# Sums of the down projection's left operand moved into the MLP's units and stored, its right operand's sums moved to VectorE, embedding stage begun ahead of the last product

## Chip, core and metric

The kernel runs on one core of a Trainium2 chip. The metric is the device time in microseconds (us): the median of three runs of the kernel before is 1584.94 us (1584.51 to 1587.78).

## What is computed

One layer of a bidirectional encoder, 1024 tokens by 1024 channels, everything in float32. What bears on the change is the second half of the layer, the gated MLP and the stage after it that adds the per-layer embedding:

```python
x = x + conv_glu(rmsnorm(x, norm_ffn_g[i]), w_ffn_gate[i], w_ffn_up[i], ffn_conv_w[i], ffn_conv_b[i], w_ffn_down[i])
gate = jax.nn.sigmoid(rmsnorm(x, norm_ple_g[i]) @ w_ple_gate[i])
x = x + (p[i] @ w_ple[i]) * gate
return rmsnorm(x, final_norm_g)

def conv_glu(h, w_gate, w_up, conv_w, conv_b, w_down):
    a, u = h @ w_gate, h @ w_up
    ap = jnp.pad(a, ((0, 0), (1, 1), (0, 0)))
    c = conv_b
    for j in range(3):
        c = c + ap[:, j:j + S] * conv_w[j]
    return (jax.nn.gelu(c, approximate=False) * u) @ w_down
```

The hidden width is 2816, that is 22 tiles of 128.

## The kernel before

**Products.** Every float32 product is made of three matmuls on a high and a low part of each operand (`mm3`). The parts are made by `split_into`: ScalarE copies the high part, then VectorE or GpSimd subtracts it from the source to get the low part (line 149 in every profile row). The MLP's products are cut into two by two blocks and made with seven block products instead of eight: from the left operand's blocks a11, a12, a21, a22 come four sums s1 to s4, from the right operand's blocks b11 to b22 four sums t1 to t4, and the products are a11·b11, a12·b21, s2·t2, s1·t1, s3·t3, s4·b22 and a22·t4. Their results are added up in the end.

**The MLP's units** (`up`, lines 1056 to 1081; `unit`, 967 to 1012). There are 11 pairs of units, each pair making two hidden tiles for all 1024 tokens: a gate unit, whose products go to PSUM banks D, D, S, S, and an up unit, on four banks E. Each unit is seven products of 12 matmuls. In a unit the banks with c22 and c12 are read by VectorE (lines 997 and 1000) before TensorE may add the last two products into the same banks. When an up unit is done, `up_done` (1038 to 1054) multiplies its two tiles by the gates (VectorE for the first half tile, GpSimd for the rest) and stores both to DRAM (`md`).

**The down projection** (`down`, 1225 to 1238; `down_chunk`, 1167 to 1223). Hidden tiles 0 and 1 (the "rest") are multiplied plainly, as four extra parts; the other 20 tiles form five blocks of four tiles. Three chunks are worked off one after the other: the first has the rest and one block (264 matmuls), the second and third have two blocks each (336 matmuls, 48 for each of the seven products). For each block `down_blocks` (1100 to 1135) loads the four a blocks from `md` (two transfers each) and the four b blocks from the weights, and forms the sums when they are asked for (line 1204): s1 to s4 on VectorE, t1 to t4 on GpSimd, all in line 1125. Then each product's two operands are split (`op_of`), the low parts on VectorE, but of the first block's b blocks and of the rest's on GpSimd. Finished banks are added by VectorE into `acc` or into the residual tiles `x` (line 1173), and in the last chunk GpSimd adds `acc` into `x` (1216 to 1220).

**The embedding stage** (`ple`, 1257 to 1353) starts when the down projection is done: for each of eight token tiles a norm, eight transposes, 48 matmuls with the gate weights, 12 with the embedding weights, and the final norm.

**What sets the order.** Each engine works its own queue in order, DMA issues on SyncE's queue (SP) too. The program's text is reordered within limits by a scheduler, and buffers of a pool are handed on when their last reader is done: pool `c` has 15 buffers of 128x1024 (a blocks, the tiles `x`, the units' outputs), pool `d` has 9 (the split operands of the down projection), `raw` has 3, `w` and `w2` hold 6 and 4 (b blocks and t sums). A load waits in SP's queue for its buffer, and all later issues stand behind it.

```python
sums = dict(s3=("a11", "a21", ALU.subtract, "a11"), s1=("a21", "a22", ALU.add, "a21"),
            s2=("a22", "s3", ALU.subtract, None), s4=("a12", "s2", ALU.subtract, "a12"),
            t1=("b12", "b11", ALU.subtract, "b11"), t3=("b22", "b12", ALU.subtract, "b12"),
            t2=("b22", "t1", ALU.subtract, None), t4=("b21", "t2", ALU.subtract, "b21"))
(v if nm[0] == "s" else p).tensor_tensor(out=t, in0=x, in1=y, op=op)
```

## Time and profile before

| | us |
|---|---|
| median of three runs | 1584.94 (1584.51 to 1587.78) |
| the profiled execution | 1580.84 |
| its span, first to last instruction | 1579.1 |
| TensorE busy in the span | 1504.4 (95%) |
| VectorE, ScalarE, GpSimd busy | 1064.5, 644.7, 611.5 |

In the span the MLP's units run from about 780 to 1205 us, the down projection from 1199 to 1446 us, and the embedding stage from there to the end. The matmul rows carry durations with their pipelining, so the time that TensorE needs for a number of matmuls is read from a stretch in which they run without a gap. "Granted clock" (PEclk) is the share of TensorE's full speed that was granted in a stretch. A time in brackets at the end of a timeline row is how long the engine had been idle, and what released it.

### The profile page before, as it was taken

The page shows a single profiled execution, that of the slowest core. Times are in us where ns is not written, and L with a number is a line of the kernel's source. Part 1 is how long each engine was busy: PE and PEld are TensorE (multiplying, and loading weights), DVE is VectorE, ACT ScalarE, POOL GpSimd, SP SyncE. Part 2 cuts the span into 40 slices and gives each one's busy share as a digit, 9 for nine tenths or more (in the row PEclk, how much of TensorE's full clock was granted, in tenths as well). Part 3 has the DMA queues.
Part 4 walks back from the last instruction along what each step waited for, and adds up shares of the span by engine and source line. Part 5 has one row for each costly group of instructions (what it writes and reads, how often), then busy time and mean ns, then how long its engine had stood idle before and what let it go on. Part 6 is the DMA issues. An engine that isn't in the chain of part 4 may idle for free.

```text
span 1579.1 us, 21704 instructions
## 1 busy us (share of the span) xinstructions
PE 1504.4 (95%) x8550; PEld 1294.9 (82%) x8550; DVE 1064.5 (67%) x1567; ACT 644.7 (41%) x1068; POOL 611.5 (39%) x406
## 2 busy tenths in 40 slices
PE   8999999999999996999999999999998989799997
PEld 7979998999799875888778888888886868687886
DVE  7355566564656666857877666666558997976665
ACT  5345535542455255514643333333333323333322
POOL 3120541243105410620577666656657250635000
PEclk9999999999999999999999999999999999899999
DMA  8100011001100110314412232222227515030011
GB/s 247 41 14 14 28 54 41 28 28 41 41 15 28 54 68 27 121 41 146 148 41 94 80 97 87 88 77 80 94 85 282 180 43 184 10 114 20 34 51 41
DMA packets 92488, 118.58 MB, mean 75 GB/s; under 512 B 5232, under 2 KB 65890, under 8 KB 92386
## 3 DMA queue, kind: packets, MB, share of 16 engines
q1 hardware_dynamic: 91954, 116.34, 22.5%
q8 instruction: 67, 1.10, 0.3%
q10 hardware_dynamic: 432, 0.86, 0.2%
q14 instruction: 35, 0.29, 0.1%
HBM read 92.01 MB, written 23.07 MB: 73 GB/s over the span
## 4 chain that ended last, share of the span: by engine, by line
PE 78%; DVE 11%; issue 4%; ACT 4%; POOL 2%; DMA 1%; DVEq 0%; ACTq 0%; POOLq 0%
PE D L156 33%; PE E L156 18%; PE S L156 9%; PE B L156 5%; PE B L495 3%; PE S L687 3%; PE B L657 3%; DVE op L149 2%; ACT e L665 2%; DVE atm L663 1%; PE S L683 1%; DVE mb L1125 1%; PE B L528 1%; DVE x L1173 1%; DVE raw L1125 1%
## 5 line engine op out<-in xcount | busy, mean ns | idle before, releaser
L156 PE MATMUL D<-w,hT 128*128 128x256 f32 x1920 | 254.8, 287 | 0.1
L156 PEld LDWEIGHTS D<-w,hT 128*128 128x128 f32 x1920 | 237.2, 192 | 2.5 <-issue 1.4
L156 PE MATMUL E<-T,S 128*128 128x512 f32 x924 | 217.2, 394 | 2.8 <-DVE S L149 1.4
L156 PEld LDWEIGHTS E<-T,S 128*128 128x128 f32 x924 | 175.1, 190 | 41.3 <-DVE S L149 1.9
L149 POOL TENSOR_TENSOR S<-w,S 128x512 fp32r<-128x512 f32 x119 | 171.6, 1456 | 92.2 <-ACT S L146 71.9
L149 POOL TENSOR_TENSOR w<-raw,w 128x1024 fp32r<-128x1024 f32 x37 | 92.1, 2493 | 275.2 <-ACT w L146 225.3
L156 PE MATMUL E<-op,op 128*128 128x512 f32 x528 | 128.6, 402 | 10.2 <-DVE x L1173 5.6
L156 PE MATMUL D<-hT,w 128*128 128x512 f32 x576 | 137.4, 394 | 0.0
L156 PEld LDWEIGHTS E<-op,op 128*128 128x128 f32 x528 | 102.9, 196 | 34.1 <-DVE x L1173 6.1
L156 PEld LDWEIGHTS D<-hT,w 128*128 128x128 f32 x576 | 106.3, 188 | 24.1 <-issue 2.9
L156 PE MATMUL S<-T,S 128*128 128x512 f32 x528 | 124.2, 389 | 1.0 <-DVE T L149 1.0
L146 ACT ACTIVATE S<-w 128x512 fp32r<-128x512 f32 x121 | 73.2, 624 | 119.2 <-PE S L156 49.5
L156 PEld LDWEIGHTS S<-T,S 128*128 128x128 f32 x528 | 99.1, 188 | 22.0 <-DVE T L149 1.4
L663 DVE TENSOR_REDUCE atm<-B 128x1 f32<-128x1024 f32 x64 | 75.3, 1218 | 42.5 <-PE B L657 42.5
L156 PE MATMUL D<-T,S 128*128 128x512 f32 x396 | 95.1, 391 | 4.1 <-ACT S L146 2.5
L156 PE MATMUL D<-w,osp 128*128 128x512 f32 x384 | 90.8, 393 | 0.0
L156 PEld LDWEIGHTS D<-T,S 128*128 128x128 f32 x396 | 74.0, 188 | 20.1 <-ACT S L146 2.7
L149 POOL TENSOR_TENSOR S<-raw,S 128x512 fp32r<-128x512 f32 x30 | 47.4, 1579 | 99.0 <-ACT S L146 99.0
L665 ACT ACTIVATE e<-B,atm 128x1024 f32<-128x1024 f32 x64 | 70.7, 1111 | 36.1 <-DVE atm L663 36.1
L156 PEld LDWEIGHTS D<-w,osp 128*128 128x128 f32 x384 | 71.1, 188 | 14.6 <-ACT osp L146 0.3
L156 PE MATMUL B<-wg,h 128*128 128x512 f32 x336 | 79.8, 394 | 0.0
L156 PEld LDWEIGHTS B<-wg,h 128*128 128x128 f32 x336 | 62.9, 189 | 13.2 <-ACT h L146 0.2
(290 smaller groups left out, 2768.7 us busy)
## 6 DMA issues: line engine op xcount, KB each, us to landing
md<-ag SPq DMA_DIRECT2D x22, 512.0 KB, 2.7
mb<-md SPq DMA_DIRECT2D x44, 256.0 KB, 3.7
raw<-in_w_in SPq DMA_DIRECT2D x40, 256.0 KB, 3.2
raw<-in_w_ffn_gate SPq DMA_DIRECT2D x20, 512.0 KB, 4.0
w<-in_w_ffn_up SPq DMA_DIRECT2D x20, 512.0 KB, 3.8
x<-in_x SPq DMA_DIRECT2D x16, 512.0 KB, 6.5
raw<-in_w_in SPq DMA_DIRECT2D x12, 512.0 KB, 3.9
w<-in_w_ffn_down SPq DMA_DIRECT2D x10, 512.0 KB, 6.3
```

What stands on the lines that cost most here:

```text
L146: nc.scalar.activation(hi, src, AF.Copy)
L149: (lo_eng or nc.vector).tensor_tensor(out=lo, in0=src, in1=f32(hi), op=ALU.subtract)
L156: m = self.nc.tensor.matmul(out, a, b, start=new and i == 0 and j == 0, stop=i == n - 1 and j == 2, skip_group_check=not new)
L495: nc.tensor.matmul(ps[:, c * 128:(c + 1) * 128], X[:, c * 128:(c + 1) * 128], vw(Y, [[2 * hh, 64 // hh], [1024 + hh, 2], [1, hh]], c * 128 ...
L528: nc.tensor.matmul(kvs[z][:, c * 128:(c + 1) * 128], KT[:, c, :], v[:, c, :], start=True, stop=True)
L657: mm = nc.tensor.matmul(scs[m][:, kk], qs[a][pr, qq], ks[b][pr, kk], start=j == 0, stop=j == 2).ins
L663: nc.vector.tensor_reduce(nm[:, m:m + 1], sc, AX.X, ALU.max, negate=True)
L665: self.last_exp = nc.scalar.activation(em, sc, AF.Exp, bias=nm[:, m:m + 1], accum_out=(s0 if m == 0 else s1)).ins
L683: nc.tensor.transpose(ps[:, i * 128:(i + 1) * 128], e[:, k * 128:(k + 1) * 128], self.ident)
L687: nc.tensor.matmul(po[:, 0:128], wT[:, k, :], v[:, k, :], start=(k == 0), stop=(k == 7))
L1125: (v if nm[0] == "s" else p).tensor_tensor(out=t, in0=x, in1=y, op=op)
L1173: v.tensor_tensor(out=to, in0=bank, in1=to, op=ALU.add)
```

## The change

The hidden tiles are paired otherwise: the two halves of the inner dimension of a block are now the first and second tile of each unit, so that a11 and a21 (first tile, token halves one and two) and a12 and a22 (second tile) all come out of one up unit.

- In `up_done` the units 1 to 10 form s1 to s4 from their own tiles in place, four VectorE subtractions or additions of 128x512 each, and store them beside a11, a12 and a22 in `md`, which has eight blocks of 128x512 for a unit: two stores of 512 KB more, and a11 is stored by itself (256 KB) instead of with a21. In place means that a sum waits for the store of the block it overwrites.
- `down_blocks` loads the seven a and s blocks instead of four, and forms only t1 to t4, on VectorE. All splits of the down projection's operands are on VectorE now.
- The first block's loads are asked for in another order, the rest's a1 and b1 with them; the tiles `x` are loaded behind them.
- In the last chunk GpSimd adds `acc` to `x` right after the product s2·t2, in another order.
- `ple` is a generator: its first part (embedding weights, the first tile's norm and transposes, the second tile's norm, the gate weights) is put into the program ahead of the last product a22·t4; half of the gate weights go into buffers of `w` and `w2` instead of `d`. The first transposes use banks E.

```diff
@@ up_done
-            self.store(out=self.md[2 * j + k], in_=out[k])
+            a11, a21 = out[0][:, 0:512], out[0][:, 512:1024]
+            md = lambda nm, n=1: self.md[j][:, BLOCKS.index(nm):BLOCKS.index(nm) + n, :]
+            if not k:
+                self.store(out=md("a11"), in_=a11)
+                if j == 0:
+                    self.store(out=md("a21"), in_=a21)
+                return
+            a12, a22 = out[1][:, 0:512], out[1][:, 512:1024]
+            self.store(out=md("a12", 2), in_=out[1].rearrange("p (b s) -> p b s", b=2))
+            if j:
+
+                v.tensor_tensor(out=a11, in0=a11, in1=a21, op=ALU.subtract)
+                v.tensor_tensor(out=a21, in0=a21, in1=a22, op=ALU.add)
+                self.store(out=md("s3", 2), in_=out[0].rearrange("p (b s) -> p b s", b=2))
+                v.tensor_tensor(out=a22, in0=a22, in1=a11, op=ALU.subtract)
+                v.tensor_tensor(out=a12, in0=a12, in1=a22, op=ALU.subtract)
+                self.store(out=md("s4", 2), in_=out[1].rearrange("p (b s) -> p b s", b=2))
@@ down_blocks
-        sums = dict(s3=("a11", "a21", ALU.subtract, "a11"), s1=("a21", "a22", ALU.add, "a21"),
-                    s2=("a22", "s3", ALU.subtract, None), s4=("a12", "s2", ALU.subtract, "a12"),
-                    t1=("b12", "b11", ALU.subtract, "b11"), t3=("b22", "b12", ALU.subtract, "b12"),
-                    t2=("b22", "t1", ALU.subtract, None), t4=("b21", "t2", ALU.subtract, "b21"))
+        sums = dict(t1=("b12", "b11", "b11"), t3=("b22", "b12", "b12"), t2=("b22", "t1", None), t4=("b21", "t2", "b21"))
...
-                    (v if nm[0] == "s" else p).tensor_tensor(out=t, in0=x, in1=y, op=op)
+                    v.tensor_tensor(out=t, in0=x, in1=y, op=ALU.subtract)
...
-            return self.op_of(get(nm), p if first and nm[0] == "b" else v)
+            return self.op_of(get(nm), v)
@@ down_chunk
-        ask("s3", "t1", "s1", "t3", "s2", "t2")
+        ask("t1", "t3", "t2", "t4")
         for i in mult(by, "s2", "t2", True):
             add(acc(i), by[i])
-        ask("s4", "t4")
+        if last:
+            for i in (4, 5, 6, 7, 0, 1, 2, 3):
...
+        prod = mult(by, "a22", "t4", False, ("a2", "b1"))
         if last:
...
-        for i in mult(by, "a22", "t4", False, ("a2", "b1")):
+
+            next(last)
+        for i in prod:
             add(xq(i, 1, 0), by[i])
@@ ple
+        nxt = norm(0)
+        hl = []
+        turner(nxt[1], hl)()
+        prev = (0, hl, nxt[0])
+        nxt = norm(1)
+        self.ple_w()
+        gbf = self.gb_load("final_norm_g", self.wf([1024]))
+        early[0] = False
+        yield
```

**Order on VectorE where a gate unit begins**, just after an up unit has ended (`ag` are a unit's outputs, `mu` its running sum, `w` and `raw` the weights of coming units). Before:

```order
L1006 TENSOR_TENSOR ag_9841<-mu_9820,E_9823 128x512
L1010 TENSOR_TENSOR ag_9842<-mu_9820,E_9824 128x512
L958 TENSOR_TENSOR w_10116<-w_10088 128x512
L959 TENSOR_TENSOR w_10116<-w_10089,w_10115 128x512
L994 TENSOR_TENSOR mu_9953<-mu_9953,D_9955 128x512
L997 TENSOR_TENSOR ag_9975<-mu_9953,S_9957 128x512
L953 TENSOR_TENSOR w_10248<-raw_10221,raw_10222 128x512
L954 TENSOR_TENSOR w_10248<-w_10248,raw_10221 128x512
L1000 TENSOR_TENSOR ag_9975<-ag_9975,S_9956 128x512
```

Of the change, at the same place of the same pair:

```order
L1008 TENSOR_TENSOR ag_9873<-mu_9852,E_9855 128x512
L1012 TENSOR_TENSOR ag_9874<-mu_9852,E_9856 128x512
L1066 TENSOR_TENSOR ag_9873<-ag_9873 128x512
L960 TENSOR_TENSOR w_10154<-w_10126 128x512
L961 TENSOR_TENSOR w_10154<-w_10127,w_10153 128x512
L996 TENSOR_TENSOR mu_9991<-mu_9991,D_9993 128x512
L1067 TENSOR_TENSOR ag_9873<-ag_9873,ag_9874 128x512
L999 TENSOR_TENSOR ag_10013<-mu_9991,S_9995 128x512
L1069 TENSOR_TENSOR ag_9874<-ag_9874,ag_9873 128x512
L1070 TENSOR_TENSOR ag_9874<-ag_9874 128x512
L1002 TENSOR_TENSOR ag_10013<-ag_10013,S_9994 128x512
```

The four sums (lines 1066 to 1070) stand between the gate unit's own reads of its banks (lines 996, 999 and 1002 now).

**Order on VectorE where the second chunk begins** (`op` are split operands, `mb` a blocks, `wf` and `w` b blocks and t sums). Before:

```order
L1125 TENSOR_TENSOR mb_11081<-mb_11081,mb_11095 128x1024
L1125 TENSOR_TENSOR raw_11107<-mb_11095,mb_10936 128x1024
L1125 TENSOR_TENSOR mb_11003<-mb_11003,raw_11105 128x1024
L149 TENSOR_TENSOR op_11011<-wf_11009,op_11011 128x1024
L1173 TENSOR_TENSOR x_10528<-D_10767,x_10528 128x512
L149 TENSOR_TENSOR op_11017<-mb_11014,op_11017 128x1024
L1173 TENSOR_TENSOR x_10530<-D_10768,x_10530 128x512
```

Of the change:

```order
L1144 TENSOR_TENSOR w_10996<-wf_11134,w_10996 128x1024
L151 TENSOR_TENSOR op_11065<-wf_11063,op_11065 128x1024
L1197 TENSOR_TENSOR x_10569<-D_10812,x_10569 128x512
L151 TENSOR_TENSOR op_11071<-mb_11068,op_11071 128x1024
L1144 TENSOR_TENSOR wf_11134<-w_11140,wf_11134 128x1024
L1144 TENSOR_TENSOR wf_11145<-w_11140,w_10996 128x1024
L1197 TENSOR_TENSOR x_10571<-D_10813,x_10571 128x512
L1144 TENSOR_TENSOR wf_11063<-wf_11063,wf_11143 128x1024
```

The s sums are gone from here and the t sums (line 1144) stand in their place, between the splits and the reads of banks D.

**Order on SP where the first chunk runs** (`raw_10561` and `raw_10622` are the rest's b1 block; `md_113` is the last unit's store). Before, the last unit's two stores and then the next chunk's blocks:

```order
L167 DMA raw_10622<-in_w_ffn_down 128x2x512
L1232 DMA x_10532<-xd_93 128x1024
L1232 DMA x_10534<-xd_94 128x1024
L1097 DMA mb_10616<-md_103 128x512
L1097 DMA mb_10616<-md_104 128x512
L161 DMA md_123<-ag_10400 128x1024
L161 DMA md_124<-ag_10401 128x1024
L1097 DMA mb_10925<-md_109 128x512
```

Of the change:

```order
L1260 DMA x_10583<-xd_90 128x1024
L169 DMA raw_10561<-in_w_ffn_down 128x2x512
L163 DMA md_113<-ag_10444 128x512
L163 DMA md_113<-ag_10445 128x1024
L163 DMA md_113<-ag_10444 128x1024
L163 DMA md_113<-ag_10445 128x1024
L1118 DMA mb_10734<-md_104 128x512
L1118 DMA mb_10734<-md_105 128x512
L1118 DMA mb_10775<-md_104 128x512
```

The first block's s2 (`mb_10734`) is issued behind the last unit's four stores, the last of which holds its s4 and s2.

## Rows read from the trace of the kernel before

**Rows 1.** Busy time by stretch in the down projection; columns in the first line.

```profile
core 0: us, PE busy (x) PEld busy (x) DVE busy (x) ACT busy (x) POOL busy (x), PEclk, DMA share, GB/s
1198.59:1445.74 247.15, 227.31 (x963) 184.56 (x961) 212.19 (x184) 79.84 (x80) 108.67 (x42) 0.95 0.35 119
...
1272.26:1294.85 22.59, 15.97 (x58) 12.31 (x57) 22.59 (x15) 6.02 (x6) 12.53 (x5) 0.85 0.01 2
...
1358.10:1381.76 23.66, 15.08 (x59) 11.49 (x57) 23.66 (x17) 6.03 (x6) 12.57 (x5) 0.81 0.05 17
```

**Rows 2.** The chain in order of time, down projection and embedding stage: start, us, work.

```profile
1295.02 10.88 PE E L156 x48
...
1465.44 0.87 PE S L1343 x8
1466.32 1.38 PE D L156 x6
```

**Rows 3.** Timeline where the second and third chunks begin: start, us, engine, instruction, [idle].

```profile
1272.70 3.27 POOL L1125 TENSOR_TENSOR wf<-w,wf 128x1024 f32<-128x1024 f32 x1
...
1273.63 3.42 DVE L1125 TENSOR_TENSOR raw<-mb,mb 128x1024 f32<-128x1024 f32 x1
...
1282.13 9.57 PE L156 MATMUL E<-op,op 128*128 128x512 f32 x30 [5.63 <-DVE x L1173]
...
1379.46 2.50 PE L156 MATMUL D<-op,op 128*128 128x512 f32 x5 [5.89 <-DVE op L149]
```

**Rows 4.** Line 1125, all its instructions: count, ns shortest/median/longest, first and last start.

```profile
L1125 DVE TENSOR_TENSOR mb<-mb,mb x10: 1224/2225/3416, 1203.4 to 1356.2; 128x1024 f32<-128x1024 f32 x10
L1125 DVE TENSOR_TENSOR raw<-mb,mb x5: 1216/3383/3424, 1223.3 to 1359.5; 128x1024 f32<-128x1024 f32 x5
L1125 DVE TENSOR_TENSOR mb<-mb,raw x5: 1205/3317/3427, 1226.8 to 1373.8; 128x1024 f32<-128x1024 f32 x5
...
L1125 POOL TENSOR_TENSOR wf<-w,w x4: 3319/3382/3396, 1264.8 to 1361.8; 128x1024 f32<-128x1024 f32 x4
```

**Rows 5.** Timeline from the last up unit to the rest's product a1·b1.

```profile
1200.18 5.78 PE L156 MATMUL E<-T,S 128*128 128x512 f32 x24
...
1217.79 1.06 ACT L146 ACTIVATE op<-mb 128x1024 fp32r<-128x1024 f32 x1 [18.56 <-DMA mb<-md]
...
1219.84 2.07 PE L156 MATMUL E<-op,op 128*128 128x512 f32 x4 [3.69 <-ACT op L146]
...
1222.39 11.95 PE L156 MATMUL E<-op,op 128*128 128x512 f32 x44 [0.47 <-POOL op L149]
```

**Rows 6.** Timeline from the last product to the first gate matmuls.

```profile
1451.63 1.97 PE L1343 MATMUL S<-cst,c 128*128 128x128 f32 x8 [2.48 <-DVE c L200]
...
1453.43 4.03 PE L156 MATMUL B<-wg,h 128*128 128x512 f32 x14
```

**Rows 7.** Busy time by stretch: one gate unit, then the up unit.

```profile
1089.79:1108.83 19.04, 19.04 (x85) 15.77 (x84) 12.17 (x12) 5.17 (x9) 13.87 (x9) 1.00 0.23 84
1108.83:1127.87 19.04, 19.04 (x85) 15.77 (x84) 13.07 (x13) 8.85 (x12) 10.89 (x7) 1.00 0.27 84
```

**Rows 8.** Timeline of that gate unit.

```profile
1094.28 2.40 POOL L1052 TENSOR_TENSOR ag<-ag,cv 128x1024 f32<-128x1024 f32 x1
1094.36 2.87 DVE L958 TENSOR_TENSOR w<-w 128x512 f32<-128x512 f32 x1 [3.31 <-POOL S L149]
...
1103.39 5.60 PE L156 MATMUL S<-T,S 128*128 128x512 f32 x24
1103.49 0.67 DVE L1000 TENSOR_TENSOR ag<-ag,S 128x512 f32<-128x512 f32 x1
...
1104.69 0.68 DVE L959 TENSOR_TENSOR w<-raw,w 128x512 f32<-128x512 f32 x1
```

**Rows 9.** The page, DMA issues: count, KB each, median us to landing.

```profile
md<-ag SPq DMA_DIRECT2D x22, 512.0 KB, 2.7
mb<-md SPq DMA_DIRECT2D x44, 256.0 KB, 3.7
```

More of the change, by code (lines that the diff above doesn't have):

```diff
@@ L89, in __init__ @@
         self.od = [pool_dram.tile([P, S], F32, name=f"od{i}") for i in range(8)]
-        self.md = [pool_dram.tile([P, S], F32, name=f"md{i}") for i in range(NF)]
+        self.md = [pool_dram.tile([P, 8, 512], F32, name=f"md{i}") for i in range(NF // 2)]
     def n(self, s):
@@ L1079, in up @@
         self.pin = None
-        for nm in ("a21", "b12", "a22", "b22"):
+        for nm in ("a1", "b1"):
+            rest(nm)
+        for nm in ("b12", "b22"):
             get(nm)
@@ L1144, in get @@
                 if nm[0] == "a":
-                    raws[nm] = self.down_m(f0, i, 0, self.c([2, 512], name="mb"))
-                else:
-                    raws[nm] = self.down_w(f0, 0, i, self.raw([2, 512]))
+                    r = raws[nm] = self.c([2, 512], name="mb")
+                    for k in range(2):
+                        self.nc.sync.dma_start(out=r[:, k, :], in_=self.md[0][:, BLOCKS.index("a%d%d" % (i + 1, k + 1)), :])
+                else:
+                    r = raws[nm] = self.raw([2, 512])
+                    self.load(out=r, in_=self.t["w_ffn_down"][0][0:256, i * 512:i * 512 + 512].rearrange("(k p) c -> p k c", p=P))
             return raws[nm]
@@ L1165, in down_mult, with down_chunk @@
                     yield i
-    def down_chunk(self, blocks, kinds, acc, rest=None, last=False):
+    def down_chunk(self, blocks, kinds, acc, rest=None, last=None):
         v = self.nc.vector
@@ L1203, in down_chunk @@
             self.prev = self.stores[-1]
-        ask("s3", "t1", "s1", "t3", "s2", "t2")
+        ask("t1", "t3", "t2", "t4")
         for i in mult(by, "s2", "t2", True):
             add(acc(i), by[i])
-        ask("s4", "t4")
+        if last:
+            for i in (4, 5, 6, 7, 0, 1, 2, 3):
+                for n in range(0 if i >= 4 else 1, 2):
+                    xs = self.xr[i][:, n * 512:n * 512 + 512]
+                    self.nc.gpsimd.tensor_tensor(out=xs, in0=xs, in1=acc(i % 4), op=ALU.add)
         bx = X()
@@ L1215, in down_chunk @@
             add(xq(i, 0, 1), bx[i])
+        prod = mult(by, "a22", "t4", False, ("a2", "b1"))
         if last:
-            for i in range(8):
-                for n in range(0 if i >= 4 else 1, 2):
-                    xs = self.xr[i][:, n * 512:n * 512 + 512]
-                    self.nc.gpsimd.tensor_tensor(out=xs, in0=xs, in1=acc(i % 4), op=ALU.add)
-        for i in mult(by, "a22", "t4", False, ("a2", "b1")):
+            next(last)
+        for i in prod:
             add(xq(i, 1, 0), by[i])
@@ L1228, in down @@
         acc = lambda i: a[i // 2][:, i % 2, :]
-        self.xr = []
-        for i in range(8):
-            xt = (self.ct if i < 2 else self.c)([1024], name="x")
-            nc.sync.dma_start(out=xt, in_=self.xd[i])
-            self.xr.append(xt)
+        self.xr = [None] * 8
+        for n, i in enumerate((4, 5, 6, 7, 0, 1, 2, 3)):
+            xt = self.xr[i] = (self.ct if n < 2 else self.c)([1024], name="x")
+            with self.after(self.loaded):
+                nc.sync.dma_start(out=xt, in_=self.xd[i])
         kinds = [self.banks_b, self.banks_ds]
         kinds = self.down_chunk([self.first_blocks], kinds, acc, self.rest)
-        kinds = self.down_chunk([self.down_blocks(f) for f in (6, 10)], kinds, acc)
-        self.down_chunk([self.down_blocks(f) for f in (14, 18)], kinds, acc, last=True)
-        self.prev = self.loaded
+        kinds = self.down_chunk([self.down_blocks(u) for u in (3, 5)], kinds, acc)
+        ple = self.ple()
+        self.down_chunk([self.down_blocks(u) for u in (7, 9)], kinds, acc, last=ple)
+        self.run(ple)
     def ple_w(self):
@@ L1247, in ple_w @@
             for kp in range(4):
-                t = self.d([2, 2, 512], F32R, "wg")
                 r0 = kp * 2 * P
+                if n:
+                    t = self.d([2, 2, 512], F32R, "wg")
+                    hi, lo = t[:, 0], t[:, 1]
+                else:
+                    hi, lo = [(self.w if kp < 2 else self.w2)([2, 512]) for _ in range(2)]
                 raw = self.raw([2, 512])
@@ L1329, in emb_T, with norm, turner @@
             return pT
-        for s in range(NS):
-            pT = emb_T(s)
-            y = self.norm_tile(self.xr[s], gb3, "n1")
-            hl = []
+        def norm(s):
+            return emb_T(s), self.norm_tile(self.xr[s], gb3, "n1")
+        def turner(y, hl):
             def turn():
@@ L1346, in turn @@
                 return tr.ins
-            if s:
-                gate(*prev, turn)
-            else:
-                turn()
+            return turn
+        nxt = norm(0)
[7 more added lines that the diff above has]
+        yield
+        for s in range(1, NS):
+            pT, y = nxt if s == 1 else norm(s)
+            hl = []
+            gate(*prev, turner(y, hl))
             prev = (s, hl, pT)
@@ L1478, in build @@
             self.down()
-            self.ple()
 def tile_net(ctx, tc, t):
```

54 lines of the change are left out of this document (29 added, 25 removed).

## The prediction

> **What bounds the kernel now.** I read the busy time of the engines by stretch first, then the chain that ended last, then the timeline where TensorE has gaps. TensorE is the bound: in the units it is busy in the whole stretch [rows 7], and the change takes away or adds hardly a matmul (eight transposes change banks). So only time in which TensorE stands idle or runs below full speed can be won.
>
> What a matmul costs: 48 without a gap take 10.88 us on the chain [rows 2], 0.2267 us each. The down projection needs 264 + 336 + 336 = 936, and 24 of a unit's own run in the same stretch: 960 x 0.2267 = 217.6 us. The stretch is 247.15 us long [rows 1] (its row lists 963, so it holds what I count). **29.5 us are lost** there. Where: at the start of the second chunk 58 matmuls stand in 22.59 us, 9.4 more than 13.15; at that of the third 59 in 23.66, 10.3 more than 13.4; the granted clock falls to 0.85 and 0.81 in both, so part of the loss is matmuls run partly at the lower of the two levels (1.2 of 2.4 GHz) after the gap [rows 1]. In the first chunk the product a1·b1 begins after a gap of 3.69 and one of 0.47, its first 4 matmuls take 2.07 for 0.91 and the next 44 take 11.95 for 9.97: together 7.3 [rows 5]. The other 2.5 are spread.
>
> Why TensorE waits at the two chunk starts: VectorE is busy for the whole of both stretches [rows 1], and TensorE is released by VectorE's adds or splits after 5.63 and 5.89 us [rows 3]. VectorE is full because its s sums meet GpSimd's t sums: 3.42 beside 3.27, begun 0.9 us apart [rows 3]. Over the stage such a sum takes 1.21 to 1.22 on VectorE at the shortest and 3.42 at the longest, and 3.38 on GpSimd [rows 4]. Twenty s sums cost some 55 us of VectorE by these rows (10 x 2.2, 5 x 3.4, 5 x 3.3), where 24 would do alone.
>
> **The change, part by part.**
>
> *S sums out, t sums on VectorE.* VectorE loses 20 sums and gets 20, at 1.22 each [rows 4], and GpSimd forms none in this stage. Nothing is left beside them that stretches them: I take 1.22, with 3.4 as the other end. At the second chunk's start VectorE's work from the last 48 matmuls of the chunk ahead until s2·t2 is 8 splits and 7 t sums at 1.22 and 8 adds at 0.68: 18.3 + 5.4 = 23.7 us. It can begin some 4 us ahead of these 48, so it is done 19.5 to 20 after their start; the 96 matmuls that TensorE has until s2·t2 take 21.8. The margin is about 2 us, and the adds come in time for the banks. So **both seams go: 9.4 + 10.3, and with the spread 2.5 and the first chunk's 7.3 all 29.5 us are won**, and what the first chunk loses in a new way is charged next. Bounds: at 3.4 us for a sum 7 of them would be 15 us late and the seams would not change at all.
>
> *The first chunk.* a1·b1 waited for the rest's operands: one released by ScalarE's copy after the load of `mb`, the other by a split on GpSimd [rows 5]. The split goes to VectorE (1.22, as line 1125 alone, the same shape) and the loads stand ahead of the tiles `x`; both gaps go. New is that s2 of the first block is loaded behind the last unit's four stores, as the order of SP shows, and the last store waits for the last sum, which stands on VectorE behind the last unit's own reads. These can begin when the unit's products end, at 1200.18 + 5.78 = 1206 [rows 5]. From there to the last sum I count 20 VectorE instructions, 5 of 128x1024 at 1.22 and 15 of 128x512 at 0.69: 16.4, so 1222. SP's issues ahead, about 2 us (chosen, 0 to 4); the transfer 3.7 [rows 9]; ScalarE's copy 1.06 [rows 5]; the split 1.22: s2·t2 can start at 1230. TensorE came to a1·b1 at 1219.84 - 3.69 = 1216.15 [rows 5], and 48 matmuls later is 1227. A gap of 3 us, and as much again at the lower clock (the rows of a1·b1: 1.2 + 2.0 after a gap of 3.69): **6 us lost**, 0 if VectorE is 3 us ahead, 10 if the issues and the landing are slow.
>
> *Loads and stores.* Transfers `mb<-md` grow from 44 to 74, of 256 KB each, stores `md<-ag` from 22 to 43, at 3.7 and 2.7 us to landing [rows 9]. In the down stretch the DMA engines are busy 0.35, moving 119 GB/s; the 30 more are 7.9 MB, 32 GB/s over it [rows 1]. I cost their volume at nothing; their place in SP's queue is a rival below.
>
> *Four sums in each up unit.* 40 sums of 128x512 stand on VectorE at the start of the following gate unit. Alone one takes 0.68, against GpSimd 2.87: the row of 2.87 stands beside GpSimd's 2.40 us multiplication and begins 0.08 after it [rows 8]. VectorE has 19.04 - 12.17 = 6.9 and 19.04 - 13.07 = 6.0 us idle in a gate and an up unit [rows 7]. They delay the reads ahead of the last two products: the second read begins 0.10 after the product ahead is done (1103.49 against 1103.39) and takes 0.67; TensorE comes back to that bank half of 5.60 later [rows 8]. So slack is 2.0 us. Two to four sums stand ahead of that read, 1.4 to 2.8 us alone, when VectorE has idle time before it; I take that most units just hold and **lose 2 us in all**; bounds 0, and 49 (a rival). Their stores cover no one's wait but the next use of `ag`; I add 0.5 for small stalls.
>
> The Trainium skill, page "SBUF — State Buffer", section "SBUF: two separate sides", speaks against these sums: the port that VectorE and GpSimd share is an exclusive lock, and the loser waits for the other's whole instruction. The row of 2.87 agrees with it: 0.68 and the 2.32 that GpSimd still had to run make 3.0. By that rule each sum could cost a whole GpSimd instruction; that is the slower rival below, whose time comes from rows.
>
> *`ple` ahead of the last product.* From the end of the last product, 1445.74, to the first gate matmuls at 1453.43 [rows 1, 6] are 7.7 us, of which TensorE worked on transposes with waits like 2.48 [rows 6]. What remains to run on TensorE there are two blocks of transposes and embedding matmuls of which the chain shows 0.87 and 1.38 [rows 2], with 0.2 between: 2.5. The last product runs 10.9 us, and the first tile's norm and transposes, which stand in the 7.7 now, fit beside it. **5.2 won**, and 0.7 as the first 14 gate matmuls take 4.03 where 14 x 0.2267 = 3.17 would do [rows 6]; 5.9 in all. Bounds: 0, if the queues of ScalarE or GpSimd hold the first tile back (gate weights' split, the adds of `acc`), and 7.7.
>
> **Sum:** -29.5 + 6 - 5.9 + 2 + 0.5 = -26.9. The profiled execution took 1580.84, 4.1 below the median of 1584.94, so 1553.9 against it and **1558 us** as a median.
>
> **The rivals.**
>
> *Late loads.* SP issues in order, and 51 more issues pass through it. If a block's load stands behind one that waits for a buffer, each chunk start keeps a gap with its slow clock after it, 7.3 as in the first chunk [rows 5], and the first chunk loses 10 instead of 6: 1558 + 14.6 + 4 = 1577. For it: a1·b1's copy waited for `mb<-md` [rows 5], and one more buffer for each block is wanted (7 a and s tiles for 4). Against: the DMA engines are two thirds idle. Chance 0.16.
>
> *Sums hold the banks (slower).* If each of the four sums in a unit begins just behind a GpSimd instruction, it takes 2.40 + 0.68 = 3.1 [rows 8], four 12.3, against 6.9 idle [rows 7]: 5.4 us over, in nine units that are followed by another: 49 in place of the 2: 1605. It decides once a unit spills more than about 3 us (27 us in nine units). For it: GpSimd is busy 13.87 of 19.04 in a gate unit [rows 7]. Against: 5.2 us of that time are free of it, and a sum delays TensorE only if it stands ahead of a bank's read. Chance 0.07.
>
> *The embedding stage gains nothing*, its first norm held back in a queue: 1558 + 5.9 = 1564. Chance 0.10.
>
> *VectorE stays the bound of the chunk starts*: sums and splits grow as in the upper bound, or the adds come late. The seams keep 19.7 and the rest of the sum is small: 1558 + 19.7 + 6 = 1584, no change. Chance 0.05.
>
> **How the numbers follow.** The forecast has 0.62, its own range 1547 (no gap in the first chunk, nothing in the units, all of 7.7 at the junction: 1558 - 6 - 2.5 - 1.8) to 1568 (first chunk 10, no gain at the junction). To leave out no more than 2 in 10 I reach to the late loads: 1547 to 1577. What a measurement of this kernel can tell from no change is 0.2%, 3 us. Faster: 0.62 + 0.16 + 0.10 = 0.88; same 0.05; slower 0.07.
>
> **What would show it.** Right: in the stretches at the second and third chunk's start TensorE shows no gap over 1 us and a granted clock of 1.00; line 1144 on VectorE takes about 1.22 in every instruction; a gap of about 3 us at the first chunk's s2·t2, released by the split of s2; the first gate matmuls follow the last product within 3 us; lines 1066 to 1070 take under 1.5 on average and gate units stay at 19.04. Wrong: a TensorE that waits in gate units for lines 999 or 1002; sums of line 1144 at 2 to 3.4 (GpSimd's adds of `acc` are the only large work left beside them); matmuls at the second or third chunk released by a transfer `mb<-md`; transposes of the first token tile that wait while the last product is over.

## The result and the profile after

The changed kernel takes **1565.05 us** (median of four runs, 1563.99 to 1566.02) against 1584.72 us of the kernel before in the same comparison: a ratio of 0.9877, 95% interval 0.9853 to 0.9902, faster by 19.7 us. The forecast was 1558, with a range from 1547 to 1577.

The profiled executions differ by less: 1566.02 against 1580.84, spans 1564.2 and 1579.1. To see where, I cut both spans at four events on TensorE's timeline: a fixed matmul just ahead of the units (757.92 before, 759.88 after), the end of the last up unit's products, the end of the last product of the down projection, the first gate matmul of the embedding stage.

| stretch, us | before | after | difference | forecast |
|---|---|---|---|---|
| up to the fixed matmul | 757.92 | 759.88 | +2.0 | 0 |
| units | 448.04 | 457.53 | +9.5 | +2 + 0.5 |
| down projection | 239.78 | 219.83 | -20.0 | -29.5 + 6 |
| last product to first gate matmul | 7.69 | 2.10 | -5.6 | -5.2 |
| embedding stage | 125.67 | 124.86 | -0.8 | -0.7 |

The first line is no effect of the change: over the fourteen profiled executions of this document it lies between 757.75 and 762.08, whatever was edited behind it. The other four lines sum to -16.9 and are what the rest of this document explains: the down projection won 3.5 us less than forecast, and the units lost 7 us more. The medians lie 2.8 us further apart than these lines; where, the two profiled executions do not show.

**The chunk starts.** Busy time by stretch in the changed kernel (columns as in [rows 1]): the whole down projection, then the last 96 matmuls ahead of s2·t2 in the second and third chunks.

```profile
1210.45:1437.24 226.79, 221.49 (x965) 182.38 (x964) 184.56 (x200) 81.34 (x84) 45.76 (x20) 0.98 0.48 165
1269.50:1291.26 21.76, 21.76 (x97) 18.02 (x96) 21.76 (x24) 8.04 (x8) 0.00 (x0) 1.00 0.35 111
1345.66:1367.42 21.76, 21.76 (x97) 18.02 (x96) 21.76 (x24) 8.04 (x8) 0.00 (x0) 1.00 0.28 87
```

Where 58 matmuls stood in 22.59 us [rows 1], 96 run in 21.76 without a gap and at the full clock. VectorE is still busy for all of it, with 24 instructions for 15, and GpSimd does nothing. All instructions of the t sums (columns as in [rows 4]):

```profile
L1144 DVE TENSOR_TENSOR w<-wf,w x4: 1217/1220/1221, 1268.2 to 1351.9; 128x1024 f32<-128x1024 f32 x4
...
L1144 DVE TENSOR_TENSOR wf<-wf,wf x4: 1219/1222/1224, 1282.6 to 1364.5; 128x1024 f32<-128x1024 f32 x4
```

1.22 us each, none stretched, as taken. Both gaps of the kernel before are gone.

**The first chunk.** Timeline of the changed kernel around s2·t2: start, us, engine, instruction, and in brackets the idle time before it and what ended it.

```profile
1222.32 11.19 SPq L163 DMA_DIRECT2D md<-ag  x3
...
1232.47 0.69 DVE L1070 TENSOR_TENSOR ag<-ag 128x512 f32<-128x512 f32 x1
1233.60 6.81 SPq L1118 DMA_DIRECT2D mb<-md  x12
...
1238.49 1.06 ACT L148 ACTIVATE op<-mb 128x1024 fp32r<-128x1024 f32 x1 [15.71 <-DMA mb<-md]
...
1240.55 1.02 PE L158 MATMUL D<-op,op 128*128 128x512 f32 x2 [2.74 <-ACT op L148]
1241.37 1.05 PE L158 MATMUL S<-op,op 128*128 128x512 f32 x2
1242.22 3.39 PE L158 MATMUL D<-op,op 128*128 128x512 f32 x10
```

This is the chain of the forecast up to its last link: SP stands 11 us at the last unit's stores, the load of s2 (`mb`) goes out when the last sum (line 1070) is done, 15.8 us behind the unit's products (16.4 in the forecast), ScalarE gets it 4.9 us later, and TensorE, released by ScalarE's copy and not by the split, has waited 2.74 us. The 14 matmuls behind it take 5.1 us (to 1242.22 + 3.39) where 3.2 would do.

**The last product.** Timeline of the changed kernel in its first quarter:

```profile
1420.57 3.36 POOL L151 TENSOR_TENSOR wg<-raw,wg 128x1024 fp32r<-128x1024 f32 x1
1421.62 3.39 DVE L151 TENSOR_TENSOR wg<-raw,wg 128x1024 fp32r<-128x1024 f32 x1
...
1424.94 0.68 DVE L1197 TENSOR_TENSOR x<-E,x 128x512 f32<-128x512 f32 x1
...
1425.67 0.69 PE L1365 MATMUL E<-cst,pr 128*128 128x128 f32 x2 [2.56 <-DVE x L1197]
1426.01 3.03 PE L158 MATMUL D<-op,op 128*128 128x512 f32 x7
```

This the forecast did not have. The embedding stage's first two transposes go to a bank E; its result is read by an add on VectorE, and that stands behind the low part of a gate weight, 3.39 us long beside one on GpSimd. The matmuls that follow the transposes in TensorE's order stand behind them: TensorE waits 2.56 us in the middle of the last product and then runs seven matmuls in 3.03 us instead of 1.6. The last product takes 15.4 us, 4.4 more than in the kernel before.

**The units.** The waits between 800 and 1200 us of the changed kernel (engine, tile and line, waited for what: us in total, times, longest). None of the three is in the kernel before.

```profile
DVE w L955 <- DMA raw<-in_w_ffn_gate: 31.1, 9, 5.0
...
ACT ag L1035 <- DMA md<-ag: 24.6, 6, 5.4
...
PE E L158 <- DVE ag L999: 5.7, 5, 2.1
```

The second row is ScalarE's wait for the stores before it may write the next `ag`. TensorE waits for line 999, as the slower rival said, but it does so in the up units (banks E), while a gate unit still takes 19.04 us (1058.94 to 1077.98 in the pair below); and VectorE is late for another reason than the sums: it stands idle for 31 us until the gate weights of the next unit arrive. Of the 9.5 us, 6.6 are waits of TensorE that the kernel before has not, 5.7 of them for line 999; behind the longest of them the granted clock is 0.51 from 1094.0 to 1097.4, close to the lower of its two levels, which is by an estimate from these figures another 1.7. Timelines of SP's queue in one pair of units, before and after, with the instructions that the late load holds up:

```profile
1040.62 0.37 SPq L167 DMA_DIRECT2D raw<-in_w_ffn_gate  x1
1055.02 3.95 SPq L161 DMA_DIRECT2D md<-ag  x2
1059.06 0.39 SPq L167 DMA_DIRECT2D raw<-in_w_ffn_gate  x1
```

```profile
1054.54 16.04 SPq L163 DMA_DIRECT2D md<-ag  x3
1070.68 1.34 SPq L169 DMA_DIRECT2D raw<-in_w_ffn_gate  x2
...
1079.26 1.30 DVE L955 TENSOR_TENSOR w<-raw,raw 128x512 f32<-128x512 f32 x1 [5.02 <-DMA raw<-in_w_ffn_gate]
...
1093.06 0.69 DVE L999 TENSOR_TENSOR ag<-mu,E 128x512 f32<-128x512 f32 x1
...
1093.89 7.32 PE L158 MATMUL E<-T,S 128*128 128x512 f32 x24 [2.15 <-DVE ag L999]
```

Before, one of the two loads goes out ahead of the pair's stores and the other 4 us behind their start. After, SP stands 16 us at the pair's first three stores, until 1066.3 for GpSimd's product and from there until 1070.2 for the second sum (line 1067), and both loads stand behind them. No wait of a sum for the store of the block that it overwrites is seen: before line 1066 VectorE waits for GpSimd's product (17.1 us in 9 places), before the other three it is not idle. The weights' own sums (lines 955 to 961) slip from the end of the gate unit to the start of the up unit, the convolution after them, and line 999 comes 2.15 us late. Why both loads stand there: `load` may put no load ahead of the sixth-last store. Six stores were three pairs of units; with four stores a pair they are one and a half.

### The profile page after: what moved, and what is told of

The parts are those of the page before. It is cut to its first block, busy times and chain, and to the rows that moved or that the text cites. A ratio compares the mean times of both kernels' runs of the same rounds, so it can differ in the third digit from the quotient of the medians.

```text
span 1564.2 us, 21892 instructions
## 1 busy us (share of the span) xinstructions
PE 1504.1 (96%) x8550; PEld 1296.2 (83%) x8550; DVE 1068.6 (68%) x1612; ACT 643.6 (41%) x1068; POOL 553.4 (35%) x381
## 4 chain that ended last, share of the span: by engine, by line
PE 68%; DVE 10%; issue 8%; POOL 7%; ACT 4%; DMA 2%; SPq 0%; DVEq 0%; POOLq 0%; ACTq 0%
PE D L158 31%; PE E L158 11%; PE S L158 6%; PE B L158 5%; POOL S L151 4%; PE B L497 3%; PE S L689 3%; PE B L659 3%; ACT e L667 2%; DVE atm L665 1%; PE S L685 1%; DMA raw<-in_w_ffn_gate 1%; POOL ag L1054 1%; POOL x L1235 1%; DVE cv L1028 1%
## 5 line engine op out<-in xcount | busy, mean ns | idle before, releaser
L151 POOL TENSOR_TENSOR S<-w,S 128x512 fp32r<-128x512 f32 x119 | 178.7, 1519 | 104.6 <-ACT S L148 98.6
L151 POOL TENSOR_TENSOR w<-raw,w 128x1024 fp32r<-128x1024 f32 x39 | 98.8, 2537 | 276.8 <-ACT w L148 225.2
L158 PE MATMUL E<-op,op 128*128 128x512 f32 x528 | 122.0, 389 | 0.0
L158 PEld LDWEIGHTS E<-op,op 128*128 128x128 f32 x528 | 99.1, 188 | 20.6
L151 POOL TENSOR_TENSOR S<-raw,S 128x512 fp32r<-128x512 f32 x30 | 51.2, 1707 | 84.6 <-ACT S L148 78.5
L148 ACT ACTIVATE w<-raw 128x1024 fp32r<-128x1024 f32 x44 | 46.6, 1059 | 75.9 <-PE D L158 59.4
L659 PE MATMUL B<-qkT,qkT 64*128 64x512 f32 x384 | 58.2, 426 | 15.0 <-ACT e L667 13.9
```

Of the source, the lines that this page charges most:

```text
L148: nc.scalar.activation(hi, src, AF.Copy)
L151: (lo_eng or nc.vector).tensor_tensor(out=lo, in0=src, in1=f32(hi), op=ALU.subtract)
L158: m = self.nc.tensor.matmul(out, a, b, start=new and i == 0 and j == 0, stop=i == n - 1 and j == 2, skip_group_check=not new)
L659: mm = nc.tensor.matmul(scs[m][:, kk], qs[a][pr, qq], ks[b][pr, kk], start=j == 0, stop=j == 2).ins
```

## The experiments

My theory after this (LOADS): the units lose their time to the place of the gate weights in SP's queue, and not (SUMS) to VectorE's time for the sums. For the down projection the question was which of its two parts closes the gaps: s sums out, or t sums off GpSimd. e1 to e4 ran beside the kernel before at 1583.14 us, e5 to e8 at 1583.11, e9 to e11 at 1582.41, e12 at 1583.99. The stretches of the profiled executions, cut as above:

| | median us | ratio (95%) | units | down | to gate | embedding |
|---|---|---|---|---|---|---|
| changed kernel | 1565.05 | 0.9877 (0.9853 to 0.9902) | 457.53 | 219.83 | 2.10 | 124.86 |
| e1 loads unpinned | 1555.47 | 0.9820 (0.9802 to 0.9838) | 447.61 | 219.76 | 2.10 | 124.88 |
| e2 no sums | 1550.77 | 0.9794 (0.9780 to 0.9808) | 448.04 | 215.37 | 2.08 | 124.92 |
| e3 t sums on GpSimd | 1574.24 | 0.9936 (0.9915 to 0.9956) | 457.12 | 227.12 | 2.10 | 125.20 |
| e4 before, t on VectorE | 1564.88 | 0.9878 (0.9863 to 0.9894) | 446.92 | 223.20 | 7.47 | 126.05 |
| e5 e1 + s2 early | 1550.45 | 0.9793 (0.9779 to 0.9806) | 446.00 | 214.87 | 2.11 | 124.90 |
| e6 e1 + transposes mid | 1555.54 | 0.9823 (0.9809 to 0.9838) | 447.59 | 215.75 | 4.68 | 126.13 |
| e7 e1, embedding late | 1557.10 | 0.9834 (0.9820 to 0.9847) | 447.60 | 215.42 | 6.44 | 126.44 |
| e8 e1, splits on GpSimd | 1558.11 | 0.9842 (0.9829 to 0.9856) | 447.57 | 215.63 | 7.90 | 125.77 |
| e9 e5 + transposes mid | 1551.57 | 0.9804 (0.9788 to 0.9819) | 447.61 | 212.19 | 4.68 | 125.24 |
| e10 e5, splits on VectorE | **1549.27** | 0.9792 (0.9779 to 0.9806) | 446.03 | 213.15 | 2.08 | 125.70 |
| e11 all three | 1552.51 | 0.9809 (0.9795 to 0.9822) | 447.59 | 212.61 | 4.69 | 125.20 |
| e12 e10, s sums back | 1555.18 | 0.9821 (0.9808 to 0.9834) | 447.59 | 218.28 | 2.11 | 124.86 |

**e1, loads unpinned.**

```diff
-            self.lag = 6
+            self.lag = 12
             self.up()
```

> The changed kernel, only that a weight load is put behind the 12th-last store instead of the 6th-last (12 stores are three pairs of units now, as 6 were before). The sums stay. Theory LOADS: the units lose time because the two loads of gate weights stand in SP's queue behind the store of s3, which waits for two sums; the first sum of gate weights (line 955) then waits for a transfer (31.1 us in 9 places), VectorE's work piles up and line 999 comes late. Then the waits at line 955 go, the wait of TensorE for line 999 goes (5.7 us in 5 places), the units lose about 10 us less, and the time is 1555 to 1557. Theory SUMS: VectorE's time for the 40 sums itself makes line 999 late. Then line 999 is waited for as before and the time stays at 1565.

1555.47 us. The units are back at 447.61, as before the change, with all 40 sums in place. In the trace of e1 the waits of line 955 for a transfer and of TensorE for line 999 are gone, and the second load is ahead of the pair's stores again:

```profile
1045.03 0.37 SPq L169 DMA_DIRECT2D raw<-in_w_ffn_gate  x1
1050.46 16.10 SPq L163 DMA_DIRECT2D md<-ag  x3
1066.66 0.39 SPq L169 DMA_DIRECT2D raw<-in_w_ffn_gate  x1
```

The stores still hold SP for 16 us; it is enough that one load of two is not behind them. ScalarE still waits 23.9 us for `ag`, now for a sum (line 1069), with the units at their full pace, so this wait is not what they lost by. From issue to landing such a load takes 3.6 us in e1 and 6.0 in the changed kernel, where the two go out together. LOADS is shown, SUMS is refuted.

**e2, no sums.**

```diff
-                v.tensor_tensor(out=a11, in0=a11, in1=a21, op=ALU.subtract)
-                v.tensor_tensor(out=a21, in0=a21, in1=a22, op=ALU.add)
...
-                v.tensor_tensor(out=a22, in0=a22, in1=a11, op=ALU.subtract)
-                v.tensor_tensor(out=a12, in0=a12, in1=a22, op=ALU.subtract)
```

> The changed kernel without the four sums in the units; s3, s1, s4 and s2 are stored as the unsummed blocks (this part of the result is left out). Theory SUMS: all that the units lost comes back, 10 us, 1555. Theory LOADS: the stores of s3 wait only for GpSimd now, so the loads behind them are about 6 us earlier than in the changed kernel but still later than in the kernel before; most comes back, 1556 to 1560, and line 955 still waits for the transfer in some places. The first chunk's gap before s2 t2 (2.74 us) should shrink in both, as the last store is not held by the sums.

1550.77 us, less than either theory had, as neither counted what the first chunk would win. The units take 448.04, as in the kernel before and 0.4 more than in e1 with the sums: the sums themselves cost the units nothing that can be seen. That all of the units' loss comes back was SUMS's forecast too, so e2 alone would not decide between the two; e1 does. The units lose only where both meet, stores that wait for sums and both loads behind them. The other 4.4 us are in the down projection, 215.37 for 219.76: with the last store not held, the first chunk's gap does not occur. From the last up unit's products to the second chunk e2 takes 58.32 us, e1 62.66 and the changed kernel 62.97. Line 955 still waits for the transfer, 5.0 us in two places, as LOADS said.

**e3, t sums on GpSimd; e4, the kernel before with its t sums on VectorE.**

```diff
-                    v.tensor_tensor(out=t, in0=x, in1=y, op=ALU.subtract)
+                    self.nc.gpsimd.tensor_tensor(out=t, in0=x, in1=y, op=ALU.subtract)
```

> The changed kernel with t1 to t4 formed on GpSimd again: only the s sums are moved. If taking the s sums off VectorE alone closes the gaps at the second and third chunk's start: GpSimd forms six t sums at up to 3.4 us, 20 us, before s2 t2, beside splits that are slowed to 2 to 3 us: gaps of 0 to 4 us each, 1565 to 1573. If the meeting of the two engines is what matters (both parts needed), the gaps come back in full, 9 to 10 each, about 1584.

```diff
-                    (v if nm[0] == "s" else p).tensor_tensor(out=t, in0=x, in1=y, op=op)
+                    v.tensor_tensor(out=t, in0=x, in1=y, op=op)
```

> The kernel before with t1 to t4 formed on VectorE: only this is moved, the s sums stay there too. If VectorE's amount of work matters: 8 splits and 14 sums at 1.22 and 8 adds at 0.68 are 32.3 us, 4 of them ahead, so 6 to 7 us beyond the 21.8 that TensorE has, and with the lower clock 8 to 9 per chunk start, 1580 to 1586. If only the meeting with GpSimd matters, the gaps close and the time is 1562 to 1566.

e3 took 1574.24, a little above the top of its first case; e4 took 1564.88, not the 1580 to 1586 of the amount of work but the 1562 to 1566 of the meeting alone. One word in the old kernel gives 18.3 us, nearly the whole of the change's 19.7. From e3, the t sums and TensorE's wait at the second chunk's s2·t2; then the same of e4 with a t sum and two s sums:

```profile
L1144 POOL TENSOR_TENSOR wf<-w,w x4: 3378/3390/3409, 1274.6 to 1362.4; 128x1024 f32<-128x1024 f32 x4
...
1295.83 1.45 PE L158 MATMUL D<-op,op 128*128 128x512 f32 x5 [1.30 <-DVE op L151]
```

```profile
L1125 DVE TENSOR_TENSOR mb<-mb,mb x10: 1214/1224/1933, 1207.6 to 1347.9; 128x1024 f32<-128x1024 f32 x10
L1125 DVE TENSOR_TENSOR raw<-mb,mb x5: 1211/1219/1225, 1224.3 to 1349.0; 128x1024 f32<-128x1024 f32 x5
...
L1125 DVE TENSOR_TENSOR wf<-w,w x4: 1219/1225/1229, 1265.2 to 1359.3; 128x1024 f32<-128x1024 f32 x4
...
1284.81 3.79 PE L156 MATMUL D<-op,op 128*128 128x512 f32 x10 [2.28 <-DVE op L149]
```

The same s sums that took 2.2 to 3.4 us [rows 4] take 1.22 as soon as GpSimd forms none beside them, and in e3, without s sums, a t sum on GpSimd still takes 3.39 beside VectorE's splits. At each chunk start TensorE's longest wait is 5.6 to 5.9 us before [rows 3], 1.3 with the s sums gone, 2.3 with the t sums moved, and none with both: each part alone does most of the work, so their gains don't add. The same by time: from the second chunk's first matmul to the last product the kernel before takes 162.4 us, e4 148.2, e3 144.7 and the changed kernel 141.4. At the chunk starts e3 is thus the better of the two; its 1574.24 comes from elsewhere. The loads of its units are pinned as in the changed kernel (457.12), and its transposes in the last product wait 5.01 us, so that this product takes 17.8.

In my count for e4 the step that failed was the cost of an instruction on a busy VectorE, as e4's timeline shows:

```profile
1264.11 1.22 DVE L1125 TENSOR_TENSOR wf<-w,wf 128x1024 f32<-128x1024 f32 x1
1265.25 1.22 DVE L1125 TENSOR_TENSOR wf<-w,w 128x1024 f32<-128x1024 f32 x1
1266.38 1.22 DVE L149 TENSOR_TENSOR op<-mb,op 128x1024 fp32r<-128x1024 f32 x1
```

Each row says 1.22 us, but they begin 1.13 to 1.14 apart, and adds 0.60: a sum of durations is too long. From the start of TensorE's last 48 matmuls of the first chunk (1259.70) to the end of the split that it then waits for (1284.76) it is 25.1 us, where I had 28.3. The head start was about the 4 us that I gave it: three of the sums stand ahead.

By the Trainium skill, page "SBUF — State Buffer", section "SBUF: two separate sides", the port that VectorE and GpSimd share is locked for a whole instruction by whichever begins first. These durations agree with it: an s sum on VectorE takes 1.22 us with no sum on GpSimd (e4) and 3.38 beside one (the median of `raw<-mb,mb` in [rows 4]).

**e5, s2 early.** On e1:

```diff
-        for nm in ("b12", "b22"):
+        for nm in ("s2", "b12", "b22"):
             get(nm)
```

> e1, and in addition the first block's s2 is asked for with the other loads, ahead of the last unit's stores (these two of its tiles were stored long before). Theory: the first chunk's gap before s2 t2 (e1: 1.96 + 0.26 us, and the matmuls behind it at the lower clock) comes from the load's place in SP's queue behind the last unit's stores, which wait for the last sums. Then the gap goes, the down projection from the last up unit's end takes about 215.4 us as in e2 and not 219.8, 4 less: 1551.5. Rival: s1, t1 or the split on VectorE is late just behind it; then the gap moves to the next product and the time stays at 1555.

1550.45 us, 5.0 less than e1, the down projection 214.87 for 219.76. Of these 4.9 us the first chunk has 3.2 (59.44 for 62.66). The other 1.7 are the last product's, 14.00 for 15.66 after a gap as long as e1's: behind it the clock did not fall in e5 (the last section comes back to this). In e5 TensorE's wait at s2·t2 is 0.70 us for 1.96 and 0.26 in e1:

```profile
1233.79 0.73 PE L158 MATMUL D<-op,op 128*128 128x512 f32 x2 [0.70 <-ACT op L148]
```

The first block comes from the second and third pairs of units, so its s2 had been in memory for long; only the place in SP's queue made it late.

**e6 to e8, the last product.** e6 puts the embedding stage's first part behind the first quarter of the last product, e7 behind all of it, e8 moves the gate weights' splits; all on e1.

```diff
-        if last:
-            next(last)
         for i in prod:
+            if last and i == 1:
+                next(last)
             add(xq(i, 1, 0), by[i])
```

> e1, and in addition the embedding stage's first part is put into the program behind the first quarter of the last product and not ahead of it. Theory: TensorE's gap of 2.54 us inside the last product, with the matmuls behind it at the lower clock (4 us in all), comes from the two transposes into a bank E that VectorE has not read yet, because of their place in TensorE's order. Then that gap goes and the first gate matmuls still follow the product within 2 to 3 us: 1551.5. Rival: the first tile's transposes become late and the 4 us move behind the product: 1555.

> e1, with the embedding stage's first part put behind the last product, as far as the order of the program goes (this undoes that part of the change). The gap in the last product goes (4 us won), and the 5.6 us that the junction won and 0.8 behind it are lost: 1557.5, that is 2 slower than e1. If the junction's gain came with the gate weights' other buffers and not with the early norm: 1551 to 1552.

```diff
-                self.split_into(hi, lo, raw, nc.gpsimd if kp % 2 else nc.vector)
+                self.split_into(hi, lo, raw, nc.gpsimd)
```

> e1, with all low parts of the gate weights formed on GpSimd and none on VectorE. Rival cause of the gap in the last product: a gate weight's split on VectorE is stretched to 3.39 us beside one on GpSimd and holds the add that frees the bank E. If so, the add comes 3 us earlier, the gap goes and the time is 1551.5 (or worse by what GpSimd has more to do before the first gate matmuls). If the place of the transposes alone decides, the gap stays at 2 to 2.5 us and the time at 1555 or above.

In all three the gap in the last product is gone and the down projection is 4.0 to 4.3 us shorter, so both its causes are shown: the transposes' place (e6) and the split ahead of the add (e8). But in all three the time comes back behind the product. e6 and e8 after the product:

```profile
1424.43 1.09 PE L1380 MATMUL E<-cst,c 128*128 128x128 f32 x8 [1.99 <-DVE c L202]
1425.77 5.33 PE L158 MATMUL B<-w,h 128*128 128x512 f32 x21 [0.25 <-ACT h L148]
```

```profile
1420.71 1.06 ACT L148 ACTIVATE wg<-raw 128x1024 fp32r<-128x1024 f32 x1 [7.45 <-DMA raw<-in_w_ple_gate]
1421.67 0.37 ACT L148 ACTIVATE pT<-E 128x256 fp32r<-128x256 f32 x1
...
1426.50 1.97 PE L1381 MATMUL E<-cst,c 128*128 128x128 f32 x8 [3.57 <-DVE c L202]
```

In e6 the first tile's norm is late (line 202), and 2.6 us are lost between product and gate: 1555.54, its rival's 1555. In e8 ScalarE waits 7.45 us for a raw gate weight, whose buffer GpSimd frees late, and the first tile's work stands behind it on ScalarE's queue: 1558.11, no better than e1. e7 undoes the early start and takes 1557.10, near its 1557.5. By the stretches it takes 4.3 + 1.6 us more behind the product and 4.3 less in it, a net of 1.6 for the early start; the intervals of e1 and e7 overlap, so that it nets anything is not shown.

**e9 to e11, together.** e9 is e5 with e6's edit. e10 is e5 with `nc.vector` for all gate weights' splits. e11 is e10 with the splits of `w_ple` on VectorE and e6's edit too.

> e5 with e6's edit as well (s2 loaded early, and the embedding stage's first part behind the first quarter of the last product). If the two savings are apart from each other and e6 saves the 1 to 2 us that its trace shows (gap of 2.5 in the product gone, 2.2 behind it come): 1549. If e6's saving is nothing, as its runs say: 1550.5.

> e5 with all low parts of the gate weights formed on VectorE. Theory MEETING: a split on VectorE takes 2.8 to 3.4 us only beside one on GpSimd; alone 1.21. Then the last product's add is late by less (three splits ahead of it at 1.2 are 3.7, against 3.4 for one now, when the two of w_ple stay on GpSimd and meet some of them), the gap in the last product is 0 to 2.5 and the norm's chain on VectorE is not slowed: 1547 to 1550. Rival AMOUNT: VectorE has four more splits ahead of the add; the gap grows by 2 to 4 us: 1552 to 1555.

> e10 with the two splits of w_ple on VectorE too and the embedding stage's first part behind the first quarter of the last product: nothing on GpSimd but its adds meets VectorE there, and no transpose waits for a bank in the product. MEETING: every split at 1.2, the first tile's transposes right behind the product: 1546 to 1548. AMOUNT: the first norm on VectorE is late behind six more splits and the gate matmuls begin 3 us later: 1552 or more.

e9 at 1551.57 (1549.07 to 1553.87) and e11 at 1552.51 win nothing that can be told on e5; in both, the 4.7 us of e6 between product and gate stand again. In e9 the last product is 2.7 us shorter than in e5 and the first gate matmul 2.6 later; the 1.6 that its units take longer stand ahead of all that the edit touches. For e11 that is the forecast of AMOUNT, but not its reason: e9 has the same wait without a split more on VectorE, so it comes with the later place. e10 is the fastest, 1549.27, though its interval covers e5's; its trace has what MEETING said, splits of 1.2 us and a wait of 0.61 where e5 has 2.47:

```profile
1409.37 1.21 DVE L151 TENSOR_TENSOR wg<-raw,wg 128x1024 fp32r<-128x1024 f32 x1
...
1409.50 0.44 PE L1365 MATMUL E<-cst,pr 128*128 128x128 f32 x2 [0.61 <-DVE x L1197]
```

**e12, s sums back.** e10, with the table of sums of the kernel before in `down_blocks` (all on VectorE), no sums in `up_done`, and the blocks stored alone.

```diff
-            self.lag = 12
+            self.lag = 9
...
-        ask("t1", "t3", "t2", "t4")
+        ask("s3", "t1", "s1", "t3", "s2", "t2")
         for i in mult(by, "s2", "t2", True):
             add(acc(i), by[i])
+        ask("s4", "t4")
```

> e10 with the s sums back in the down projection on VectorE, beside the t sums, as in e4; the blocks a11, a21, a12, a22 are stored alone, a weight load stands behind the ninth-last store (three pairs), the first block's a blocks are loaded ahead of the last unit's stores. What the moving of the s sums itself is worth once the t sums are on VectorE: by e4's trace 2.3 us of gap at each of two chunk starts, with the lower clock 3 to 4 each, so 1555 to 1557. Rival: nothing, since VectorE catches up: 1549 to 1550.

1555.18 us, the 1555 to 1557 forecast and not the rival: moving the s sums is worth 5.9 us once the t sums are on VectorE (4.3 if each median is set against the kernel before beside it). In the traces the second and third chunks take 5.9 us more and the first, whose s2 no longer waits for a store, 1.3 less; and e12's trace has the gaps of e4 again, 2.39 and 2.28 us:

```profile
1282.31 2.56 PE L158 MATMUL D<-op,op 128*128 128x512 f32 x10 [2.39 <-DVE op L151]
1361.04 2.56 PE L158 MATMUL D<-op,op 128*128 128x512 f32 x10 [2.28 <-DVE op L151]
```

## Why the prediction was right, and where it was not

- **What bounds the kernel, and why TensorE waited at the chunk starts: right.** The gaps came from the meeting of s sums and t sums (e3, e4), both are gone, and line 1144 takes the 1.22 us that was taken for it.
- **The 2 us of margin at the chunk starts: right only in its sign.** In the trace of the changed kernel VectorE does the 8 splits, 7 sums and 8 adds of the count between 1269.36 and 1291.26, and at 1291.26 TensorE comes to s2·t2: no idle time is left on VectorE, and no wait results. Two errors met. VectorE had one sum ahead (at 1268.23, against 1269.50 for the last 48 matmuls), 1.3 us and not 4; and the work took 21.9 us and not 23.7, as its instructions begin closer together than their durations add up to (e4). How near to a wait this is no run shows. The two parts of the change are each worth most of the gap, where I had costed them as one: the t sums alone give some 18 us, the s sums 4 to 6 on top (e12).
- **The first chunk, 6 us lost: right in mechanism, a little large.** It lost 4.6, 62.97 us against the 58.32 of e2. The gap was the forecast's (2.74 for 3); behind it 1.9 were lost and not as much again.
- **"ple ahead of the last product", 5.9 won: right for what lies behind the product** (6.4 in the table above), but the term was one-sided. That the transposes need a bank whose add on VectorE stands behind a stretched split was not costed; it takes 4.4 back in the changed kernel (e6 to e8 win 4.0 to 4.3 by removing it, and lose it behind the product), and what the part nets, 1.6 by e7, is not clear of the runs' spread.
- **"Four sums in each up unit", 2 us lost: the step that failed.** The units lost 9.5. The step looked at VectorE's idle time and the slack of the bank reads, and there it was right: with the loads moved the sums cost nothing (e1). Its signs came out too, a gate unit takes 19.04 and lines 1066 to 1070 take 1.36 on average; they watched the gate units, and the loss came in the up units. What it left out stands in two other steps. "Loads and stores" named the place in SP's queue a rival, but only for the chunk starts; in the units a store waits for GpSimd's product and then 4 us for two sums, and the count of stores also sets how far ahead a weight may be loaded. That was in `load` and `up_done` to be read.
- **The rivals.** Late loads (0.16) were the mechanism that decided, in a place that I had not given them. The slower rival had the right symptom, TensorE waiting for line 999, and the wrong cause.

The differences against the sum: units and small stalls +7.0 (9.5 for 2.5), last product +4.4, the rest of the down projection -0.8, behind the product -0.5, together +10. -26.9 + 10 = -16.9, the sum of the stretches. The two large errors have the same sign and are whole mechanisms left out; that 1565 still lies in the range is owed to room kept there for other terms (the first chunk, the junction), which is luck.

## What to carry to other kernels

Before moving large sums off VectorE, look at what GpSimd does beside them: where both read two operands of SBUF at once, giving all of it to VectorE can be faster than sharing, as one word did here for 18 us. Count the work of a busy engine by the starts of successive rows and not by the durations that they show. A step that adds stores to an in-order DMA queue has to be followed through that queue: which loads stand behind a store that now waits for arithmetic, and which constants of the program count stores. Work put ahead of its time on TensorE's queue waits in order; cost the wait of its first instruction, and what its own preparation does to the engine that releases it.

## What was not expected of the hardware

A busy share of 1.00 on VectorE for 21.76 us, at both chunk starts, costs TensorE nothing in the changed kernel; the kernel before had the same share with 15 instructions for 24, and waits.

Not all of VectorE's work stretches beside GpSimd. In e3 the adds that read one operand from a bank of PSUM keep their 0.68 us beside a t sum; the splits around them, with both operands in SBUF, take 2.83 and 3.42:

```profile
1278.96 3.42 DVE L151 TENSOR_TENSOR op<-wf,op 128x1024 fp32r<-128x1024 f32 x1
1281.37 3.27 POOL L1144 TENSOR_TENSOR wf<-w,wf 128x1024 f32<-128x1024 f32 x1
1282.30 0.68 DVE L1197 TENSOR_TENSOR x<-D,x 128x512 f32<-128x512 f32 x1
1282.90 2.83 DVE L151 TENSOR_TENSOR op<-mb,op 128x1024 fp32r<-128x1024 f32 x1
```

A gap of about the same length was followed by another clock. Busy time by stretch around the two transposes, in the changed kernel (gap 2.56) and in e5 (gap 2.47):

```profile
1421.82:1431.64 9.82, 7.26 (x28) 5.65 (x26) 7.15 (x7) 2.21 (x4) 3.18 (x2) 0.83 0.28 82
```

```profile
1407.10:1415.49 8.39, 5.92 (x27) 4.60 (x26) 8.18 (x14) 2.37 (x4) 4.43 (x2) 1.00 0.30 96
```

The granted clock is 0.83 in the one and 1.00 in the other, and the seven matmuls behind the gap take 3.03 and 1.87 us. What decides that no run here tells apart, so a gap can cost its own length or some 2 us more: of the forecast's "as much again at the lower clock" the changed kernel lost 1.9 us behind its gap of 2.74, and e5 hardly anything behind its 2.47.
